# Prompt values of the sparse and memory attention as pairs of 64-column matmuls, two transposed buffers at a time

## Chip, core and metric

The kernel runs on one core of one Trainium2 chip. The metric is the device time of one launch in microseconds (us), and lower is better. "PE" is TensorE's matrix engine, "PEld" its weight loads, "DVE" VectorE, "ACT" ScalarE, "POOL" GpSimd, and "SP" the queue that issues nearly all of the DMAs.

## What is computed

The reference is one layer with three groups of heads side by side, for a prompt of 2048 tokens and for a sample batch of 8 sequences of 16 new tokens with a cache of 4096 keys. The change touches the last step of groups B and C for the prompt: probabilities times values.

```python
def sparse_block(q, qi, wi, q_pos, k, v, ki, k_pos, n_sel):      # group B, 4 heads of 64
    ...                                                          # top-256 of an indexer's scores
    s = jnp.einsum('bqhd,bqkhd->bqhk', q, ks) * (B_HD ** -0.5)
    p = jax.nn.softmax(s, axis=-1)
    return jnp.einsum('bqhk,bqkhd->bqhd', p, vs)

# group C, 4 heads of 64, 256 memory tokens
s_m = jnp.einsum('bqhd,bmhd->bhqm', q_m, mem_k) * (M_HD ** -0.5)
o_m = jnp.einsum('bhqm,bmhd->bqhd', jax.nn.softmax(s_m, axis=-1), mem_v)
o_m = o_m.reshape(bsz, t_len, M_WIDTH) * jax.nn.silu(z_m)

mix = jnp.concatenate([o_a, o_b, o_m], axis=-1)
y = x + mix @ w_out
```

## The kernel before

The 2176 tokens are 17 tiles of 128: tile 0 holds the sample's tokens, tiles 1 to 16 the prompt's. A first stage (up to about 1540 us) does the projections, group A and the indexer's selection. The second stage, the function `attention` (line 1677), does the rest, and the change lies in it. Several generators describe the work of that stage, and `weave` (line 173) interleaves them: each call of an engine through `Paced` (line 147) adds that class's own estimate of its duration to a clock, and the generator whose clock stands lowest is asked next. A Tile scheduler then fixes the order on each engine, so that one order of instructions per engine and per queue goes to the chip, and an engine waits at the next instruction of its list until that one can start.

The generators that matter here:

- `scores()` (line 1763) makes, for prompt tile g, the scores of 4 heads against 128·g keys and their exponentials in tiles `Sm`, and the scores against the memory in `Smm`.
- `values()` (line 1816) takes them up. A block is 128 queries by 128 keys of one head. Four blocks (two heads h, two key blocks c) are transposed on PE (`pt<-cf,Sm`, one call of 128x128 each), copied by ACT or DVE in turn into a buffer `PT` (two such buffers), and then multiplied with the values `Vt` (`mvt` for the memory). The multiplication is one call a key block: 128 value columns, which are two heads of 64, against 256 columns of `PT`, which are the probabilities of both heads. The result is 128x256, and half of it (one head's values under the other head's probabilities) is never read. The products of a buffer are queued behind the next buffer's transposes (the variable `late`). `hp` counts pairs of heads, `part` is 0 for group B and 1 for the memory.
- `outputs()` (line 1910) multiplies with `w_out` (`py<-woh,mixh` and so on, 24 calls a tile) once `values()` has stored a tile's `mixT`. It runs over the prompt tiles 1 to 16 and last over tile 0, the sample's, which it can start when the sample is done.
- `sample()` (line 1462) streams the sample's cache in 72 steps: 4 pairs of sequences with 17 key pieces each, and then 4 steps for the memory. A step has scores (`py` or `pi<-skt,bd`), an exponential, two transposes (`<-cf,SP`), a copy into `sPT`, and values two steps later (`<-svt,sPT`). These matmuls are 32 columns wide and lie in four column groups of the array. After the 68th and after the 72nd step the rows are gathered back out of a scratch tensor: 32 small DMAs `sPT<-os_d` on SP (line 1656), then a product with the gate and a store to `mix_d` (line 1660). The gather overwrites the tile `sPT` that the next step's copy needs.

Of the kernel before, what the change touches and what calls it, by code (L numbers as in the profile page):

```python
# [5 lines left out]
F32 = mybir.dt.float32  # L6
# [3 lines left out]
AF = mybir.ActivationFunctionType  # L10
OP = mybir.AluOpType
# [195 lines left out]
def build(tc, nc, a):  # L207
# [3 lines left out]
    V, S, G, T = (Paced(e, n, log) for e, n in ((nc.vector, "V"), (nc.scalar, "S"), (nc.gpsimd, "G"), (nc.tensor, "T")))  # L211


    cpool = ctx.enter_context(tc.tile_pool(name="const", bufs=1))
# [6 lines left out]
    ident = C("ident")  # L221
# [31 lines left out]
                                            ("glog", "beta", "gc", "ngc", "egc", "esuf", "last"))  # L253
    lasts = cpool.tile([128, 32], F32, name="lasts")
    hist = cpool.tile([128, 12, 3], F32, name="hist")
    Sst = cpool.tile([128, 4, 128], F32, name="Sst")
    V.memset(Sst, 0.0)
    cw = cpool.tile([128, 48], F32, name="cw")
    nc.sync.dma_start(cw, a["conv_w"])
    V.tensor_scalar(cw, cw, 0.5, None, op0=OP.mult)  # L260
# [21 lines left out]
    wpool = b1.enter_context(tc.tile_pool(name="wpool", bufs=2, side="right"))  # L282
    spool = b1.enter_context(tc.tile_pool(name="small", bufs=2))
    gpool = b1.enter_context(tc.tile_pool(name="gains", bufs=1))
    gains = gpool.tile([128, 224], F32, name="gains")
    nc.sync.dma_start(gains, a["gains"].to_broadcast([128, 224]))
    for o in (0, 128):
# [5 lines left out]
    po = b1.enter_context(tc.tile_pool(name="po", bufs=1, space=PSUM))  # L293
# [89 lines left out]
    def together(ins):  # L383

        return ExitStack() if ins is None else tc.issue_after(ins.ins)
# [865 lines left out]
    hp = b1.enter_context(tc.tile_pool(name="hp", bufs=2))  # L1251
# [55 lines left out]
    for gi in range(len(GROUPS)):  # L1307
        t = [[t_step(4 * gi + h, 0), t_step(4 * gi + h, 1)] for h in range(4)]
        n = [n_step(gi, pi) for pi in (1, 0, 2, 3, 4, 5)]
        steps += [i_step(gi)] + t[0] + n[:1] + t[1] + n[1:3] + t[2] + n[3:4] + t[3] + n[4:]  # L1310
    loaded, ready = [], []
# [365 lines left out]
    def attention(first):  # L1677
        with ExitStack() as b3:
# [5 lines left out]
            op = pool(b3, "op", 1, side="right")  # L1684
            py = pool(b3, "py", 2, side="right", space=PSUM)
            kv = pool(b3, "kv", 1)
            ap = pool(b3, "ap", 1)
            pt_ = pool(b3, "pt", 2, space=PSUM)
            ps_ = pool(b3, "ps", 1, space=PSUM)
            po_ = pool(b3, "po", 1, space=PSUM)  # L1690
# [5 lines left out]
            ready = []  # L1696
            M = sample_tiles(sp)
            sms = Slots(*((ap, "Sm%d" % i) for i in range(NS)))
            HALF = 1024

            class sx:
                name = "sx"
# [113 lines left out]
            def values():  # L1816


                for g in range(1, NT):
                    rows = slice(128 * g, 128 * g + 128)  # L1820
                    gate = ap.tile([128, 512], F32, name="gate")
                    nc.sync.dma_start(gate, gate_d[rows, :])
                    mixT = ap.tile([128, 4, 128], F32, name="mixT")
                    for part in range(2):
                        po = po_.tile([128, 512], F32, name="po").rearrange("p (a q) -> p a q", q=256)
                        nb = (g, 2)[part]
                        for hp in range(2):
                            j = 5 * (g - 1) + (4 if part else 2 * hp + 1)
                            yield from until(lambda: len(ready) > j)
                            yield -ready[j]["at"]  # L1830
                            if part:
                                blocks = [(h, c, ready[j]["x"][0][0][0][:, (2 * hp + h) * 256 + 128 * c:][:, :128], mvt[:, c])
                                          for c in range(2) for h in range(2)]
                            else:
                                blocks = [(h, c, ready[j - 1 + h]["x"][0][128 * c // HALF][0][:, 128 * c % HALF:][:, :128], Vt[:, c])
                                          for c in range(g) for h in range(2)]
                            late = None
                            for i in range(0, len(blocks) + 4, 4):
                                b = blocks[i:i + 4]
                                if b:  # L1840
                                    pt = pt_.tile([128, 4, 128], F32, name="pt")
                                    for x, (_, _, P, _) in enumerate(b):
                                        T.transpose(pt[:, x, :], P, ident)
                                    c = b[-1][1]
                                    if not part and ((c + 1) * 128 % HALF == 0 or c == g - 1):
                                        sms.free += [ready[j - 1 + h]["x"][0][128 * c // HALF][1] for h in range(2)]
                                    PT = ap.tile([128, 4, 128], F32, name="PT", bufs=2)
                                    if i // 4 % 2:
                                        V.tensor_copy(PT[:, :len(b)], pt[:, :len(b)])
                                    else:  # L1850
                                        S.activation(PT[:, :len(b)], pt[:, :len(b)], AF.Copy)
                                    yield 1
                                if late:
                                    yield 1
                                    for x, (_, c, _, Vb) in enumerate(late[0][::2]):
                                        T.matmul(po[:, hp], Vb[:, 128 * hp:128 * hp + 128], late[1][:, 2 * x:2 * x + 2, :].rearrange("p h q -> p (h q)"),
                                                 start=c == 0, stop=c == nb - 1, skip_group_check=True)
                                    yield 1
                                late = (b, PT)
                            count["v"] += hp if part else 2  # L1860
                        j = 5 * (g - 1) + (4 if part else 3)
                        den = ready[j]["x"][1]
                        V.reciprocal(den, den)
                        V.tensor_scalar(den, den, 0.5, None, op0=OP.mult)
                        gp = gate[:, 256 * part:256 * part + 256]
                        g3 = gp.rearrange("p (h d) -> p h d", d=64)
                        V.tensor_tensor(g3, g3, den[:, :, None].to_broadcast([128, 4, 64]), op=OP.mult)
                        yield 1
                        pt = pt_.tile([128, 4, 128], F32, name="pt")
                        for i in range(2):  # L1870
                            T.transpose(pt[:, i, :], gp[:, 128 * i:128 * i + 128], ident)
                        yield 1
                        mp = mixT[:, 2 * part:2 * part + 2]
                        S.activation(mp, pt[:, :2], AF.Copy)
                        yield 1
                        for h in range(2):
                            r = slice(64 * h, 64 * h + 64)
                            V.tensor_tensor(mp[r], po[r, :, 128 * h:128 * h + 128], mp[r], op=OP.mult)
                    nc.sync.dma_start(mixT_d[512:, rows].rearrange("(k p) t -> p k t", p=128), mixT)
                    count["o"] = g  # L1880

# [106 lines left out]
```

## Time and profile before

| What | Value |
|---|---|
| Median of 3 runs | 2322.36 us (2319.55 to 2326.96) |
| The profiled execution | 2319.37 us, of which 2317.5 us is the span from the first to the last instruction |
| PE busy over the span | 2041.4 us (88%), 13451 matmul instructions |
| PEld / DVE / ACT / POOL busy | 73% / 72% / 56% / 18% |
| Mean granted TensorE clock | 0.944 of full speed |
| DMA | 453.17 MB, 196 GB/s in the mean |
| The second stage's values, `po<-PT,Vt` | 544 instructions, 146.4 us busy |

An fp32 call stands as two MATMUL instructions in the profile, so the 544 instructions are 272 calls. A matmul's end is modelled: consecutive ones overlap in the rows, so the time that one costs is read from the start of one to the start of the next. The profile gives no chain of work that ended last for this kernel, so the path has to be read from starts and waits.

### The profile page before, as it was taken

What the parts mean: (1) busy time and instruction counts of PE and PEld (TensorE: products, weight loads), DVE (VectorE), ACT (ScalarE), POOL (GpSimd) and SP (SyncE); (2) the same over time, 40 slices, a digit from 0 to 9 for tenths busy, and PEclk for the clock granted to TensorE, in tenths of its full rate; (3) what the DMA queues carried; (4) which work ended last, traced back from release to release, by engine and by line L of the source; (5) the groups of instructions that cost most, each with busy time, mean ns of one, the idle gap of its engine ahead of it and who ended that gap; (6) DMA issues with size and microseconds to landing.
All of it is one profiled execution on the core that took longest, in us unless ns stands there. A gap on an engine that the chain in (4) does not pass through costs nothing.

```text
span 2317.5 us, 42207 instructions
## 1 busy us (share of the span) xinstructions
PE 2041.4 (88%) x13451; PEld 1682.0 (73%) x13451; DVE 1672.7 (72%) x6603; ACT 1293.4 (56%) x3193; POOL 420.7 (18%) x494
## 2 busy tenths in 40 slices
PE   4877878788899998999899999989999989999897
PEld 3655646677688987888788888856677666777675
DVE  4766655576888788889898897777677786646552
ACT  3455555455545565666666664457557666545441
POOL 3232413111111111111121012133111221110000
PEclk9987979798999998999899999999999999999898
DMA  7687667775544546556555656367777766766321
GB/s 233 181 250 212 215 149 236 193 249 188 196 161 164 177 154 233 182 192 226 184 206 178 227 195 218 119 201 245 237 222 236 237 215 222 244 217 193 109 65 61
DMA packets 323528, 453.17 MB, mean 196 GB/s; under 512 B 81760, under 2 KB 230880, under 8 KB 303840
## 3 DMA queue, kind: packets, MB, share of 16 engines
q1 hardware_dynamic: 322976, 449.32, 61.1%
q8 instruction: 109, 1.79, 0.3%
q0 software_dynamic: 320, 1.06, 0.3%
q14 instruction: 123, 1.01, 0.1%
HBM read 344.53 MB, written 105.75 MB: 194 GB/s over the span
## 4 chain that ended last, share of the span: by engine, by line


## 5 line engine op out<-in xcount | busy, mean ns | idle before, releaser
L169 PE MATMUL pp<-wh,xh 128*128 128x256 f32 (+1 forms) x952 | 287.3, 302 | 8.6 <-ACT xh L169 3.6
L169 PE MATMUL pp<-wl,xh 128*128 128x256 f32 (+1 forms) x952 | 278.7, 293 | 2.2 <-POOL wl L169 2.2
L169 PE MATMUL pp<-wh,xl 128*128 128x256 f32 (+1 forms) x952 | 277.9, 293 | 1.7 <-DVE xl L169 1.7
L169 PE MATMUL pp<-xh,wh 128*128 128x384 f32 (+1 forms) x640 | 249.2, 389 | 7.7 <-ACT q L169 3.0
L169 ACT ACTIVATE relu<-pi 128x512 f32<-128x512 f32 (+3 forms) x340 | 183.5, 545 | 117.5 <-PE pi L169 70.6
L169 PE MATMUL pp<-xh,wl 128*128 128x384 f32 (+1 forms) x640 | 242.7, 380 | 2.7 <-DMA wl<-wd2l 1.7
L169 DVE SCALAR_TENSOR_TENSOR score<-relu,w,score 128x512 f32<-128x512 f32 (+3 forms) x304 | 220.8, 728 | 31.6 <-ACT relu L169 18.0
L169 PE MATMUL pp<-xl,wh 128*128 128x384 f32 (+1 forms) x640 | 242.4, 379 | 0.0
L169 PEld LDWEIGHTS pp<-wh,xh 128*128 128x128 f32 x952 | 184.2, 194 | 12.8 <-ACT xh L169 5.1
L169 PEld LDWEIGHTS pp<-wl,xh 128*128 128x128 f32 x952 | 184.4, 194 | 5.7 <-POOL wl L169 2.6
L169 PEld LDWEIGHTS pp<-wh,xl 128*128 128x128 f32 x952 | 183.5, 193 | 4.8 <-DVE xl L169 2.6
L169 ACT ACTIVATE junk<-score,tf 128x1024 bf16<-128x1024 f32 (+11 forms) x126 | 142.6, 1132 | 72.0 <-DVE tf L169 47.1
L169 PE MATMUL po<-PT,Vt 128*128 128x256 f32 x544 | 146.4, 386 | 0.5 <-ACT PT L169 0.3
L169 POOL TENSOR_TENSOR Lm<-Lp,cf 128x256 f32<-128x256 f32 (+1 forms) x120 | 85.4, 712 | 312.1 <-PE pb L169 289.0
L169 PE MATMUL pi<-kstack,qst 128*128 128x512 f32 (+3 forms) x304 | 128.5, 431 | 14.6 <-ACT relu L169 12.1
L169 PEld LDWEIGHTS pp<-xh,wh 128*128 128x128 f32 x640 | 125.6, 196 | 17.5 <-ACT q L169 3.7
L169 PEld LDWEIGHTS pp<-xh,wl 128*128 128x128 f32 x640 | 125.3, 196 | 15.0 <-POOL wl L169 2.2
L169 PE MATMUL py<-woh,mixh 128*128 128x512 f32 x272 | 123.9, 456 | 12.2 <-ACT mixh L169 12.0
L169 PEld LDWEIGHTS pp<-xl,wh 128*128 128x128 f32 x640 | 125.8, 197 | 8.2
L169 POOL TENSOR_TENSOR wl<-wr,wh 128x512 fp32r<-128x512 f32 (+1 forms) x61 | 80.4, 1328 | 214.3 <-ACT wh L169 198.4
L169 PE MATMUL py<-woh,mixl 128*128 128x512 f32 x272 | 111.0, 409 | 3.5 <-POOL mixl L169 3.3
L169 PEld LDWEIGHTS po<-PT,Vt 128*128 128x128 f32 x544 | 95.3, 190 | 21.2 <-issue 6.7
(421 smaller groups left out, 5490.7 us busy)
## 6 DMA issues: line engine op xcount, KB each, us to landing
skt<-in_kT SPq DMA_DIRECT2D x128, 256.0 KB
svt<-in_v SPq DMA_DIRECT2D x128, 256.0 KB
nraw<-in_x SPq DMA_DIRECT2D x34, 256.0 KB
xres<-in_x SPq DMA_DIRECT2D x34, 256.0 KB
part_d<-xres SPq DMA_DIRECT2D x34, 256.0 KB
xres<-part_d SPq DMA_DIRECT2D x34, 256.0 KB
out_y<-xres SPq DMA_DIRECT2D x34, 256.0 KB
mixr<-mixT_d SPq DMA_DIRECT2D x33, 256.0 KB
```

What stands on the lines that cost most here:

```text
L169: return f(*args, **kw)
```

## The change

`visit` queues the products of up to two buffers in one run, and `tc.issue_after` (through `together`) ties the second buffer's run behind the first's. A product is now one head: 64 value columns against the 128 columns of that head's probabilities, written to partitions 0 to 63 (h = 0) or 64 to 127 (h = 1) of `po`. So each 128x256 call becomes two 64x128 calls that lie in different halves of the array's columns. There are three `PT` buffers instead of two, products are queued when three buffers wait, and what is left over at the end of a part is queued then; the list `late` now runs over both pairs of heads. The product with the gate is one instruction of 128x256 instead of two of 64x256. `Sst` moves to a pool that is closed before the second stage.

```diff
-    Sst = cpool.tile([128, 4, 128], F32, name="Sst")
-    V.memset(Sst, 0.0)
...
+    Sst = gpool.tile([128, 4, 128], F32, name="Sst")
+    V.memset(Sst, 0.0)
...
+                def visit(po, nb, late, n):
+                    lead = None
+                    for hp, b, PT in late[:n]:
+                        with together(lead):
+                            for x, (h, c, _, Vb) in enumerate(b):
+                                d = 64 * (2 * hp + h)
+                                ins = T.matmul(po[64 * h:64 * h + 64, hp, :], Vb[:, d:d + 64], PT[:, x, :],
+                                               start=c == 0, stop=c == nb - 1, skip_group_check=True)
+                        lead = ins
+                    del late[:n]
...
-                        po = po_.tile([128, 512], F32, name="po").rearrange("p (a q) -> p a q", q=256)
+                        po = po_.tile([128, 512], F32, name="po")[:, :256].rearrange("p (a q) -> p a q", q=128)
                         nb = (g, 2)[part]
+                        late = []
...
-                            late = None
-                            for i in range(0, len(blocks) + 4, 4):
+                            for i in range(0, len(blocks), 4):
...
-                                    PT = ap.tile([128, 4, 128], F32, name="PT", bufs=2)
+                                PT = ap.tile([128, 4, 128], F32, name="PT", bufs=3)
...
-                                if late:
-                                    yield 1
-                                    for x, (_, c, _, Vb) in enumerate(late[0][::2]):
-                                        T.matmul(po[:, hp], Vb[:, 128 * hp:128 * hp + 128], late[1][:, 2 * x:2 * x + 2, :].rearrange("p h q -> p (h q)"),
-                                                 start=c == 0, stop=c == nb - 1, skip_group_check=True)
-                                    yield 1
-                                late = (b, PT)
+                                late.append((hp, b, PT))
+                                yield 1
+                                if len(late) > 2:
+                                    visit(po, nb, late, 2)
+                                    yield 1
                             count["v"] += hp if part else 2
+                        yield 1
+                        visit(po, nb, late, len(late))
+                        yield 1
...
-                        for h in range(2):
-                            r = slice(64 * h, 64 * h + 64)
-                            V.tensor_tensor(mp[r], po[r, :, 128 * h:128 * h + 128], mp[r], op=OP.mult)
+                        V.tensor_tensor(mp, po, mp, op=OP.mult)
```

The order of the whole second stage moves, on every engine. Three places of it follow; `po` are the products in question, `pt<-cf,Sm` the transposes ahead of them, `svt`, `skt` and `SP` the sample's values, scores and transposes, `py<-wo` the output's products.

On PE, in the values of the last prompt tile (g = 16), before:

```order
L169 MATMUL po<-PT,Vt 128x256
L169 MATMUL ps<-mkst,qm 128x256 x4
L169 MATMUL po<-PT,Vt 128x256
L169 MATMUL pt<-cf,Sm 128x128 x4
L169 MATMUL po<-PT,Vt 128x256 x2
```

and in the changed kernel:

```order
L169 MATMUL po<-PT,Vt 64x128 x8
L169 MATMUL pt<-cf,Sm 128x128
L169 MATMUL pi<-skt,bd 32x256 x2
L169 MATMUL pt<-cf,Sm 128x128 x7
L169 MATMUL po<-PT,Vt 64x128 x8
L169 MATMUL pt<-cf,Sm 128x128 x4
```

Four transposes were followed by two products before; now up to eight narrow products stand together, and steps of the sample stand between them. Counted over the second stage, the 336 calls stood in 183 runs before, and the 672 narrow ones stand in 139 runs, of which 39 are whole runs of 8.

On PE, the end of the program from the last prompt tile's memory values on, before:

```order
L169 MATMUL pt<-cf,Smm 128x128 x8
L169 MATMUL pt<-cf,gate 128x128 x2
L169 MATMUL po<-PT,mvt 128x256 x4
L169 MATMUL py<-woh,mixh 128x512
L169 MATMUL py<-wol,mixh 128x512
```

and in the changed kernel:

```order
L169 MATMUL po<-PT,mvt 64x128 x8
L169 MATMUL pt<-cf,gate 128x128 x2
L169 MATMUL pi<-svt,sPT 32x128 x8
L169 MATMUL pi<-skt,bd 32x256 x4
L169 MATMUL pi<-cf,SP 128x128 x2
L169 MATMUL py<-woh,mixh 128x512
```

Before, the sample's last step stood two prompt tiles ahead of this place; now its last four steps stand behind it, the first of them ahead of the last prompt tile's output products.

On SP, around the second gather of the sample's rows, before:

```order
L1656 DMA sPT<-os_d 16x64 x28
L1657 DMA sPT<-gate_d 128x256
L1900 DMA xres<-part_d 128x512
L1822 DMA gate<-gate_d 128x512
L1660 DMA mix_d<-sPT 128x256
```

and in the changed kernel, from the first gather on:

```order
L1656 DMA sPT<-os_d 16x64 x31
L1657 DMA sPT<-gate_d 128x256
L1887 DMA mixT_d<-mixT 128x4x128
L1660 DMA mix_d<-sPT 128x256
L1929 DMA mixr<-mixT_d 128x4x128
```

Before, three prompt tiles' stores (`mixT_d`) still followed the second gather; now the last prompt tile's store stands behind the first gather, and nothing but the last stores and loads of the output follow the second one.

## Rows read from the trace of the kernel before

**Rows 1.** Windows: length; busy us of PE, PEld, DVE, ACT, POOL; granted clock; DMA share; GB/s.
```profile
1573.00:2140.00 567.00, 537.95 (x4094) 400.18 (x4094) 393.49 (x1313) 338.23 (x848) 92.17 (x82) 0.99 0.72 227
2140.00:2180.00 40.00, 31.06 (x218) 22.65 (x216) 18.65 (x61) 15.69 (x42) 3.26 (x3) 0.84 0.40 120
2180.00:2287.00 107.00, 103.27 (x593) 83.79 (x591) 55.36 (x152) 48.31 (x97) 6.38 (x5) 1.00 0.21 65
2287.00:2318.00 31.00, 15.17 (x54) 11.28 (x54) 4.32 (x8) 1.23 (x2) 1.27 (x1) 0.77 0.23 80
```

**Rows 2.** Waits of PE from 1573 to 2290 us: total, times, longest.
```profile
PE py L169 <- DMA svt<-in_v: 7.9, 8, 3.0
PE po L169 <- ACT PT L169: 1.3, 2, 1.0
```

**Rows 3.** The tiles `po` and `PT`: count, shortest, median and longest ns.
```profile
L169 PE MATMUL po<-PT,Vt x544: 377/379/535, 1573.6 to 2282.9; 128*128 128x256 f32 x182
L169 PE MATMUL po<-PT,mvt x128: 377/379/484, 1583.0 to 2286.5; 128*128 128x256 f32 x128
...
L169 ACT ACTIVATE PT<-pt x112: 361/597/628, 1573.1 to 2284.7; 128x512 f32<-128x512 f32 x104, 128x256 f32<-128x256 f32 x8
L169 DVE COPY PT<-pt x64: 411/685/693, 1607.0 to 2281.4; 128x512 f32<-128x512 f32 x56, 128x256 f32<-128x256 f32 x8
```

**Rows 4.** Timeline of PE: start us, length, instruction, count.
```profile
1902.39 1.02 PE L169 MATMUL po<-PT,Vt 128*128 128x256 f32 x4
1903.26 0.38 PE L169 MATMUL py<-cf,SP 128*128 128x128 f32 x2
1903.47 0.60 PE L169 MATMUL pt<-cf,qs 128*128 128x128 f32 x4
...
1907.28 0.64 PE L169 MATMUL py<-svt,sPT 128*32 128x128 f32 x16
1907.74 0.29 PE L169 MATMUL py<-smask,selb 128*32 128x256 bf16 x4
1907.85 0.61 PE L169 MATMUL py<-skt,bd 128*32 128x256 f32 x8
1908.40 1.13 PE L169 MATMUL po<-PT,Vt 128*128 128x256 f32 x4
```

**Rows 5.** Timeline of PE, the sample's values of steps 68, 69 and 72.
```profile
2150.06 0.43 PE L169 MATMUL pi<-svt,sPT 128*32 128x128 f32 x8 [1.32 <-ACT sPT L169]
...
2171.69 1.77 PE L169 MATMUL pi<-svt,sPT 128*32 128x128 f32 x14 [5.11 <-ACT sPT L169]
...
2188.94 0.64 PE L169 MATMUL pi<-svt,sPT 128*32 128x128 f32 x16
```

**Rows 6.** Timeline of SP's queue over the two gathers.
```profile
2153.79 0.38 SPq L1649 DMA_DIRECT2D os_d<-sO  x1
...
2171.25 0.32 SPq L1660 DMA_DIRECT2D mix_d<-sPT  x1
...
2192.22 14.07 SPq L1656 DMA_DIRECT2D sPT<-os_d  x28
...
2209.16 0.32 SPq L1660 DMA_DIRECT2D mix_d<-sPT  x1
```

**Rows 7.** Timeline of PE from the last values to the end.
```profile
2284.97 1.90 PE L169 MATMUL po<-PT,mvt 128*128 128x256 f32 x8
2294.00 0.80 PE L169 MATMUL py<-woh,mixh 128*128 128x512 f32 x1 [7.13 <-ACT mixh L169]
...
2302.85 0.60 PE L169 MATMUL pt<-cf,mixr 128*128 128x128 f32 x4
2304.19 0.50 PE L169 MATMUL py<-woh,mixh 128*128 128x512 f32 x1 [0.75 <-ACT mixh L169]
...
2309.86 0.19 PE L169 MATMUL pf<-cf,fail 128*1 128x1 f32 x2
```

**Rows 8.** Timeline of SP's queue, the last prompt tile's store.
```profile
2287.90 0.37 SPq L1879 DMA_DIRECT2D mixT_d<-mixT  x1
```

More of the change, by code (lines that the diff above doesn't have):

```diff
@@ L1836, in values @@
                                           for c in range(g) for h in range(2)]
-                            late = None
-                            for i in range(0, len(blocks) + 4, 4):
+                            for i in range(0, len(blocks), 4):
                                 b = blocks[i:i + 4]
[L1840 to L1846, printed above, removed]
-                                    PT = ap.tile([128, 4, 128], F32, name="PT", bufs=2)
[L1848 to L1851, printed above, removed]
-                                    yield 1
-                                if late:
-                                    yield 1
-                                    for x, (_, c, _, Vb) in enumerate(late[0][::2]):
-                                        T.matmul(po[:, hp], Vb[:, 128 * hp:128 * hp + 128], late[1][:, 2 * x:2 * x + 2, :].rearrange("p h q -> p (h q)"),
-                                                 start=c == 0, stop=c == nb - 1, skip_group_check=True)
-                                    yield 1
-                                late = (b, PT)
@@ new lines, in values @@
+                                pt = pt_.tile([128, 4, 128], F32, name="pt")
+                                for x, (_, _, P, _) in enumerate(b):
+                                    T.transpose(pt[:, x, :], P, ident)
+                                c = b[-1][1]
+                                if not part and ((c + 1) * 128 % HALF == 0 or c == g - 1):
+                                    sms.free += [ready[j - 1 + h]["x"][0][128 * c // HALF][1] for h in range(2)]
+                                PT = ap.tile([128, 4, 128], F32, name="PT", bufs=3)
@@ new lines, in values @@
+                                if i // 4 % 2:
+                                    V.tensor_copy(PT[:, :len(b)], pt[:, :len(b)])
+                                else:
+                                    S.activation(PT[:, :len(b)], pt[:, :len(b)], AF.Copy)
+                                late.append((hp, b, PT))
+                                yield 1
+                                if len(late) > 2:
+                                    visit(po, nb, late, 2)
+                                    yield 1
```

## Prediction

> **What bounds the kernel now.** The change lies in the second stage, so the first view is the table of windows. From 1573 us, when the prompt's values begin, to 2140 us PE is busy for 537.95 of 567 us (95%), and from 2180 to 2287 for 103.27 of 107 us (97%), at a granted clock of 0.99 and 1.00; DVE stands at 69% and ACT at 60% in the first of these, the DMA engines at 0.72 [rows 1]. So the stage moves at PE's pace. The second view, PE's waits, agrees: a few us on the sample's loads (7.9 us on `svt`), 1.3 us on the copies of transposed probabilities [rows 2]. Two short stretches are otherwise. Between 2140 and 2180 PE is busy for only 31.06 of 40 us and the clock is 0.84 [rows 1]: this is the end of the sample, where a copy into `sPT` waits for the gather and PE waits 5.11 us for the copy [rows 5, 6]. And the last 31 us after the last values are a chain of DMA, copy and products [rows 1, 7, 8], with PE half idle.
>
> **What a product costs, before and after.** The tile view counts 544 + 128 instructions, which are 336 calls at two each [rows 3]. Four of them in a row take from 1902.39 to 1903.26, 0.87 us, so a call of 256 columns takes 0.435 us, and all 336 take 146.2 us of PE [rows 4]. A narrow call streams 128 columns: 0.218 us if it stands alone. There are 672 of them, so all is lost unless two run at once. No row shows 64-column matmuls in two halves, but the sample's 32-column ones show four groups at once. Its 16 `svt` instructions are 8 calls of 128 columns; in file they would take 8 x 0.218 = 1.74 us, and they take 0.46 us, from 1907.28 to 1907.74, which is two rounds of 0.23 us [rows 4]. Its 8 `skt` instructions are 4 calls of 256 columns and take 0.55 us instead of 1.74 us, one round and 0.115 us [rows 4]. I therefore take 0.23 us for a round of two narrow calls, and the bounds are 0.218 us (nothing on top) and 0.435 us (one after the other). I choose the near end because these rows are of the same engine, type and column count.
>
> The 672 calls stand in 139 runs, and a run with an odd number wastes half a round: 367 rounds by count over the order shown above. They cost 367 x 0.23 = 84.4 us. Besides, the array changes between 128-wide and narrower use at each end of a run. Counted the same way, the changes of width rise from 224 to 455. The `skt` run carries 0.115 us beyond its one round, and 0.012 us of that is in the `svt` rounds too, so I take 0.10 us a change, with 0 and 0.2 us as bounds, since a change to 64 columns is in no row: 231 x 0.10 = 23.1 us. **PE gets 146.2 - 84.4 - 23.1 = 38.7 us back.**
>
> **The smaller parts.** One product with the gate in place of two of 64 partitions takes some 0.42 us off DVE 32 times; DVE is not what PE waits for, so I count it as nothing, and were that cover gone it would be worth 13 us at most. The copies into `PT` stay the same 112 on ACT and 64 on DVE at about 0.60 and 0.69 us [rows 3]. Their waits (1.3 us [rows 2]) stay or shrink: with three buffers a product begins further behind the transpose that it needs. A third buffer and the move of `Sst` cost no instruction in the stage. The front of the program up to 1573 us is the same.
>
> **What moves to the end.** This is the part that decides how much of the 38.7 us is seen. Before, the sample's last step ran at 2188.94, some 96 us before the last values ended at 2284.97 + 8 x 0.2175 = 2286.7 [rows 5, 7]. Now the prompt runs ahead of the sample in the order, and the sample's last four steps, its two gathers and its output stand behind the last values, where nothing covers them. Two gains come with that. Four steps of 1907.28 to 1908.40, 1.1 us each [rows 4], leave the front: 4.5 us. And the hole of 2140 to 2180 leaves it: PE was idle for 8.9 us there, where 5% would be 2, and the clock was low for a part [rows 1]; I take 11 us, between 7 and 13. So the last values end 38.7 + 4.5 + 11 = **54.2 us earlier**, at 2232.5.
>
> The end itself I add up from the rows. From the values of step 68 to those of step 69 it took 2150.06 to 2171.69, 21.6 us, for the first gather [rows 5]. From step 69 to step 72 it took 17.3 us, to 2188.94, with other products in between [rows 5]; here about half of the 24 output products stand there, at 0.23 us, so I take 13 us, between 9 and 17. From step 72 to the store of the gathered rows: 2188.94 to 2209.16, 20.2 us, of which 14.07 us are 28 DMA issues [rows 5, 6]. From such a store to the product that reads it: 2287.90 to 2294.00, 6.1 us [rows 7, 8]; the sample's has transposes in front, from 2302.85 to 2304.19, 1.3 us with a copy of some 0.7 us that the 6.1 hold already [rows 7], so 6.7 us. The 24 products after such a pause took 2294.00 to 2302.85, 8.9 us [rows 7]. From their end at 2309.86 to the end of the span: 7.6 us [rows 7]. Together 78.0 us from step 68. Step 68 stands ahead of the last values by 16 rounds, 26 transposes at 0.105 us [rows 4], a `skt` round of two halves and a dozen changes of width, about 9 us. So from the last values to the end it will be 69.0 us, where it was 2317.5 - 2286.7 = 30.8 us: **the end gets 38.2 us longer.**
>
> **The sum.** -54.2 + 38.2 = -16 us. Against the profiled execution, 2319.4 us, this is 2303.4 us, rounded 2303; the median of the runs shown lies 3 us higher than that execution.
>
> **Rivals.**
> *Pairs that overlap less (slower).* The place is each round of two 64-column calls. The point from which it decides: the front must save 38.2 us to pay for the longer end, so the rounds may cost 146.2 - 23.1 + 15.5 - 38.2 = 100.4 us, 0.274 us each. A pair that takes longer makes the kernel slower; at 0.33 us (half overlapped) it is 121 us and the kernel 2324 us; with no overlap at all the rounds cost 146.2 us and it ends near 2365 us. For it: two halves are in no row. Against it: four quarters overlap fully. TensorE: Matmul & The Clock Gate (the Trainium skill, Measured speedup vs the span model) gives 2.38 times for three column tiles, 0.79 of full; by that ratio a round would take an estimated 0.275 us and the kernel would stay where it is, and the `svt` row above speaks against it. Chance 0.13.
>
> *The room is not taken (no change).* PE's 38.7 us come back as idle time, because the sample's loads, DVE and the copies cannot run faster: 16 us of new waits, out of more than 650 us, are enough to end at 2319 us. For it: 7.9 us of waits on `svt` already, the DMA share of 0.72, DVE 69% [rows 1, 2]. Against it: PE is the one engine near full, and the sample's steps are now spread over a longer part of the stage. PSUM Bottleneck in TensorEngine Tiling (the Trainium skill) warns that evacuation becomes the limit once matmuls speed up; here the copies are 112 x 0.6 + 64 x 0.69 = 111 us on two engines over 714 us [rows 3]. Chance 0.17.
>
> *A shorter end (faster by more).* The waits on `svt` go (7.9 us), steps 69 to 72 take 9 us, and changes of width cost half: 8 + 4 + 12 us more, 2279 us. Chance 0.08.
>
> That the sample would not be last in spite of the order is excluded, since each engine follows its list.
>
> **How the numbers follow.** My forecast (PE saves about 39 us, the bare end takes back about two thirds of what the front gains) has a chance of 0.62; with 0.08 for the shorter end the kernel is faster with 0.70. A measurement of this kernel can tell 0.3% (7 us) from no change: unchanged 0.17, slower 0.13. The range begins a little below the shorter end, at 2276 us, and goes up to 2326 us, which takes in the unchanged case and the half overlapped pair; changes of width at 0.2 us would add 23 us to the forecast and reach the same end. No overlap lies outside.
>
> **What would show it.** Right: `po` instructions in pairs a few ns apart, runs of 8 calls in about 0.95 us; the last `po<-PT,mvt` near 2232 us; then a PE that waits some 12 us on `sPT` for the first gather, and again about 25 us between the sample's last values and its output's transposes, at a low granted clock; and some 69 us from the last values to the end. Wrong: pairs 0.2 us apart; more idle time of PE between 1600 and 2200 us than the 5% of before; or a sample whose last steps stand well ahead of the last values.

## The result and the profile after

| What | Value |
|---|---|
| Median of the changed kernel | 2284.4 us (2283.38 to 2285.57, 4 runs) |
| Median of the kernel before beside it | 2320.95 us (4 runs) |
| Ratio | 0.9838, 95% interval 0.9816 to 0.986, which is 33 to 43 us less |
| Profiled execution of the changed kernel | 2285.57 us, span 2283.8 us |

The kernel is faster by 36.5 us where 16 was forecast. The direction was right, and so were the overlap of the pairs and the longer end. What the new order does to the stage ahead of the last values was put far too low.

The windows of the changed kernel come first; the columns are as in [rows 1]. The second stage begins at 1575 us here, 2 us later than before, and the last values end at 2220.

```profile
1575.00:2140.00 565.00, 547.46 (x4747) 399.98 (x4750) 397.07 (x1333) 360.71 (x882) 97.24 (x83) 0.99 0.70 220
2140.00:2180.00 40.00, 38.86 (x367) 27.09 (x359) 23.39 (x70) 21.23 (x53) 2.56 (x2) 1.00 0.54 170
...
1575.00:2220.00 645.00, 623.68 (x5469) 454.11 (x5469) 439.50 (x1464) 397.00 (x975) 101.61 (x87) 0.99 0.68 214
2220.00:2283.00 63.00, 23.34 (x142) 14.82 (x142) 9.78 (x32) 4.24 (x11) 1.28 (x1) 0.70 0.24 74
```

PE is busy for 547.46 of 565 us, 97% where it was 95% [rows 1], and the hole of 2140 to 2180 is gone. From the first values to the last it is idle for 645 - 623.68 = 21.3 us. Before, the same stretch showed:

```profile
1573.00:2287.00 714.00, 672.28 (x4901) 506.63 (x4900) 467.50 (x1525) 402.24 (x986) 101.81 (x90) 0.98 0.62 196
```

That is 714 - 672.28 = 41.7 us of idle time. I call the first stretch the *front* and the rest up to the span's end the *end*. The front went from 712.9 to 644.2 us (first `po<-PT` to last, the latter from 2286.5 to 2219.7), and the end from 31.0 to 64.1 us.

The products in the tile view, which answers to [rows 3] (1088 + 256 instructions, 672 calls), and in the timeline of PE, which answers to [rows 4]:

```profile
L169 PE MATMUL po<-PT,Vt x1088: 272/273/476, 1575.5 to 2217.2; 128*64 128x128 f32 x182
L169 PE MATMUL po<-PT,mvt x256: 272/273/323, 1585.1 to 2219.7; 128*64 128x128 f32 x128
```

```profile
1993.89 0.40 PE L169 MATMUL py<-woh,mixh 128*128 128x512 f32 x1
1994.12 0.39 PE L169 MATMUL py<-wol,mixh 128*128 128x512 f32 x1
1994.35 0.40 PE L169 MATMUL py<-woh,mixl 128*128 128x512 f32 x1
1994.67 1.09 PE L169 MATMUL po<-PT,Vt 128*64 128x128 f32 x16
1995.70 0.54 PE L169 MATMUL pi<-svt,sPT 128*32 128x128 f32 x12
...
2208.97 0.43 PE L169 MATMUL po<-PT,Vt 128*64 128x128 f32 x2
2209.33 0.66 PE L169 MATMUL pt<-cf,Sm 128*128 128x128 f32 x4
...
2214.05 1.09 PE L169 MATMUL po<-PT,Vt 128*64 128x128 f32 x16
2215.07 0.66 PE L169 MATMUL pt<-cf,Sm 128*128 128x128 f32 x4
2215.66 0.66 PE L169 MATMUL po<-PT,Vt 128*64 128x128 f32 x8
2216.25 0.44 PE L169 MATMUL pi<-cf,SP 128*128 128x128 f32 x2
```

Eight calls take 1.02 us and four take 0.59 us (2214.05 to 2215.07, 2215.66 to 2216.25). The difference, 0.43 us, is two rounds, so a round of two calls costs 0.215 to 0.218 us and the pairs overlap in full; in the trace the instructions of a pair start 6 to 7 ns apart. What is left of a run is 1.02 - 4 x 0.218 = 0.15 us, and the product in front of a run takes 0.32 us instead of 0.23 (1994.35 to 1994.67). So a run carries 0.24 us, 0.12 us for each of its two changes of width.

The end in the timeline of PE, which answers to [rows 5, 7], and then in SP's queue [rows 6, 8]:

```profile
2210.52 0.43 PE L169 MATMUL pi<-svt,sPT 128*32 128x128 f32 x8
...
2218.83 1.14 PE L169 MATMUL po<-PT,mvt 128*64 128x128 f32 x16 [0.31 <-ACT PT L169]
2219.91 0.44 PE L169 MATMUL pt<-cf,gate 128*128 128x128 f32 x2
2232.73 1.77 PE L169 MATMUL pi<-svt,sPT 128*32 128x128 f32 x14 [12.39 <-ACT sPT L169]
...
2243.17 0.65 PE L169 MATMUL pi<-svt,sPT 128*32 128x128 f32 x16
...
2266.10 1.11 PE L169 MATMUL pt<-cf,mixr 128*128 128x128 f32 x4 [19.10 <-DMA mixr<-mix_d]
2267.96 0.79 PE L169 MATMUL py<-woh,mixh 128*128 128x512 f32 x1 [0.75 <-ACT mixh L169]
...
2275.59 0.19 PE L169 MATMUL pf<-cf,fail 128*1 128x1 f32 x2
```

```profile
2214.10 15.32 SPq L1656 DMA_DIRECT2D sPT<-os_d  x31
...
2246.25 11.94 SPq L1656 DMA_DIRECT2D sPT<-os_d  x26
...
2261.21 0.33 SPq L1660 DMA_DIRECT2D mix_d<-sPT  x1
```

The end runs as forecast: after the last values PE waits 12.39 us for the copy behind the first gather, whose 31 issues occupy the queue for 15.32 us, and later 19.10 us for the sample's rows, with the second gather's issues in it.

### The profile page after: what moved, and what is told of

Same layout as the page of the kernel before. It is cut to its first block, busy times and chain, and to the rows that moved or that the text cites. A ratio compares the mean times of both kernels' runs of the same rounds, so it can differ in the third digit from the quotient of the medians.

```text
span 2283.8 us, 43471 instructions
## 1 busy us (share of the span) xinstructions
PE 2006.2 (88%) x14123; PEld 1637.8 (72%) x14123; DVE 1651.3 (72%) x6571; ACT 1290.8 (57%) x3193; POOL 421.6 (18%) x494
## 4 chain that ended last, share of the span: by engine, by line
## 5 line engine op out<-in xcount | busy, mean ns | idle before, releaser
L169 PE MATMUL py<-wol,mixh 128*128 128x512 f32 x272 | 110.3, 405 | 0.0
L169 POOL TENSOR_TENSOR mixl<-mixr,mixh 128x512 fp32r<-128x512 f32 x33 | 42.3, 1281 | 328.1 <-ACT mixh L169 252.3
```

Source lines behind the costliest of these rows:

```text
L169: return f(*args, **kw)
```

## The experiments

On the chips of the experiments the unchanged first stage took 1579 to 1591 us and the kernel before 2332 to 2337 us. So totals are compared by their ratio to the kernel before on the same chip, and the traces by the lengths of front and end.

| Kernel | Ratio (95%) | Front | idle in it | End |
|---|---|---|---|---|
| before | 1 | 712.9 | 41.7 | 31.0 |
| changed | 0.9838 (0.9816 to 0.986) | 644.2 | 21.3 | 64.1 |
| wide_two | 0.9924 (0.9895 to 0.9953) | 684.1 | 26.1 | 42.5 |
| wide_order | 0.9956 (0.9925 to 0.9986) | 674.2 | 25.9 | 62.9 |
| narrow_one | 0.9956 (0.9931 to 0.9981) | 702.0 | 45.8 | 30.9 |
| in_file2 | 0.9963 (0.9941 to 0.9985) | 663.6 | 14.0 | 63.6 |
| fewer_stops | 1.0106 (1.0069 to 1.0142) | 646.9 | 18.5 | 129.5 |
| more_stops | 0.987 (0.9826 to 0.9915) | 686.0 | 42.3 | 31.7 |
| one_gather | 0.9771 (0.9736 to 0.9806) | 640.7 | 22.0 | 45.0 |
| mem_gather | 0.9721 (0.9689 to 0.9753) | 641.9 | 22.9 | 31.9 |
| before_gather | 0.9928 (0.9903 to 0.9953) | 707.4 | 36.9 | 30.8 |
| after_again (the changed kernel) | 0.9859 (0.9825 to 0.9894) | 645.7 | 24.4 | 64.1 |
| mg_y1 | 0.9775 (0.974 to 0.981) | 653.8 | 27.9 | 32.7 |
| three_all | 0.9735 (0.9699 to 0.977) | 648.4 | 28.0 | 31.7 |

Times in us. Where a text below turns a ratio into a time, it is the ratio times 2321 us. Front, idle time and end come from one traced execution of each kernel, up to 10 us away from that kernel's median (mg_y1: 2272 against 2282 us; wide_order: 2327 against 2322), and the rows of before and of the changed kernel were taken apart from the others, where before ran 0.5 to 0.7% slower. So differences of a few us between fronts are not told from noise.

### Is it the pairs or the queueing?

**wide_two** keeps the queueing and the third buffer and goes back to wide calls (with the `po` tile and the product with the gate as before):

```diff
-                            for x, (h, c, _, Vb) in enumerate(b):
-                                d = 64 * (2 * hp + h)
-                                ins = T.matmul(po[64 * h:64 * h + 64, hp, :], Vb[:, d:d + 64], PT[:, x, :],
+                            for x, (_, c, _, Vb) in enumerate(b[::2]):
+                                ins = T.matmul(po[:, hp], Vb[:, 128 * hp:128 * hp + 128], PT[:, 2 * x:2 * x + 2, :].rearrange("p h q -> p (h q)"),
...
```

> The changed kernel with its queueing (two buffers in a run, three buffers), but each product again one call of 128 x 256. Theory A (the gain is TensorE time of the narrow pairs, plus idle time that falls because the sample's steps are spread otherwise): the products cost 146 us again instead of about 106 with their changes of width, so some 38 us more than the changed kernel; the sample's last step has 6 wide products and 48 output products behind it, where the changed kernel has 0 and 37, so the end is a few us shorter: about 2318 us (2308 to 2328), as before. Theory B (the idle time falls because of the narrow pairs, in any order): 2340 to 2350 us. Theory C (the queueing and the third buffer bring the gain, the narrow pairs nothing): 2280 to 2292 us.

Measured: 0.9924, 17.6 us faster than before, between what theories A and C expected. So A was wrong in one point: the queueing brings something by itself. The front is 28.8 us shorter, 15.6 of it idle time, and the end 11.5 us longer.

**wide_order** writes the same wide calls but enters the narrow calls' estimate into `weave`, so that the order is nearly the changed kernel's (of the 4262 other matmul instructions of the stage 3778 stand in the same sequence on PE):

```diff
-                                ins = T.matmul(po[:, hp], ...
+                                ins = nc.tensor.matmul(po[:, hp], ...
...
+                                log.extend([("T", 214.0 * 0.62 + 3)] * 2)
...
```

> The changed kernel in its very order, but two narrow calls at a time are one call of 128 x 256 at the same place. Theory A: idle time stays at the changed kernel's 21 us up to the last values, the products cost 38 to 40 us more: about 2322 us (2316 to 2330). Theory B: the idle time goes back to before's 49 us: about 2349 us. Theory C: about 2284 us, as the changed kernel.

Measured: 0.9956, 2311 us, below what theory A expected (2316 to 2330) and far from B and C. The windows:

```profile
1588.00:2262.00 674.00, 648.15 (x4794) 499.94 (x4793) 460.86 (x1494) 399.11 (x975) 100.38 (x87) 0.99 0.65 204
2262.00:2324.00 62.00, 25.18 (x143) 15.59 (x142) 10.20 (x33) 3.74 (x10) 1.28 (x1) 0.71 0.25 75
```

Idle time in the front is 674 - 648.15 = 25.9 us without a single narrow product: it fell with the order, as A said and B denied. Against this kernel, the changed one's front is 28 to 30 us shorter (644.2 and 645.7 against 674.2) at an end that is 1 us longer; by the ratios the difference is 23 to 27 us (0.9859 and 0.9838 against 0.9956). That is what the pairs bring in an order that is nearly held fixed.

**narrow_one** puts the narrow pairs into the kernel before, one buffer at a time:

```diff
-                                    for x, (_, c, _, Vb) in enumerate(late[0][::2]):
-                                        T.matmul(po[:, hp], Vb[:, 128 * hp:128 * hp + 128], late[1][:, 2 * x:2 * x + 2, :].rearrange("p h q -> p (h q)"),
+                                    for x, (h, c, _, Vb) in enumerate(late[0]):
+                                        d = 64 * (2 * hp + h)
+                                        T.matmul(po[64 * h:64 * h + 64, hp, :], Vb[:, d:d + 64], late[1][:, x, :],
...
```

> The kernel before with narrow pairs, its queueing of one buffer at a time and two buffers kept. Some 60 more runs of products than in the changed kernel, so about 119 more changes of width at 0.093 us, 11 us more of TensorE; but the sample's last step has 124 narrow products and 91 output products behind it, so the end would be the 31 us of before and not 64. Theory A (idle time stays as before, 49 us): 2284 + 11 - 33 + 27 = 2289 us (2280 to 2298). Theory B (idle time falls as in the changed kernel): about 2262 us (2255 to 2270). Theory C (narrow pairs bring nothing): 2320 us or more.

Measured: 0.9956, which is 2311 us, 10 us faster than before and not 30: a miss for A (2280 to 2298) and B (about 2262). C's 2320 is nearest, but lies outside the interval (2305 to 2317). Idle time stays high at 45.8 us, as A said, and the end at 30.9. What A had wrong is the front: 702.0. This kernel has 575 changes of width where before had 224; at 0.12 us, 351 more cost 42 us, and 370 rounds cost 80.7 us, so of the 146.2 us of before only 23 are saved, and 11 of them show in the front, where idle time is also 4 us higher. My expectation counted from the changed kernel, whose front also holds the order's gain, and took only the idle time out of it. So pairs pay little when every buffer is a run of its own.

**in_file2** sorts the calls of a run by half:

```diff
-                    for hp, b, PT in late[:n]:
...
+                    flat = sorted(((hp, x, *v, PT) for hp, b, PT in late[:n] for x, v in enumerate(b)), key=lambda v: v[2])
```

> The changed kernel with the calls of a run sorted by the half of the array that they use, all of the lower half, then all of the upper: neighbours share a half and only one pair in a run can overlap, about 214 rounds of 0.22 us more. Theories A and B: 45 to 48 us more than the changed kernel, about 2331 us (2320 to 2340); a run of 8 calls takes some 1.65 us instead of 1.02. Theory C: no difference, 2284 us.

Measured: 0.9963, 24 to 29 us more than the changed kernel (0.9859 and 0.9838) where 45 were expected. A run of eight calls in this kernel's timeline:

```profile
2002.00 1.58 PE L169 MATMUL po<-PT,Vt 128*64 128x128 f32 x16
2003.51 0.65 PE L169 MATMUL pt<-cf,Sm 128*128 128x128 f32 x4
```

It takes 1.51 us, against 1.02 us with the halves in turn and 1.65 us expected: neighbours in one half go one after the other, but the upper half's calls begin while some of the lower half's are left (in the trace of this run single starts some 0.11 us apart up to 2002.49, then starts of both halves up to 2002.87, then single ones again). Theory C, that the pairs bring nothing, falls here and with wide_order.

### Is it the order?

After these four I held theory D: the pairs save some 30 us of PE, and the queueing's own effect is the order. `values()` stops less often, so `weave` lets the prompt run ahead of the sample; the sample's steps are spread over more of the front, and what PE no longer waits for there comes back as the bare end.

**fewer_stops** is the kernel before with two stops per buffer taken out and nothing else:

```diff
                                 if late:
-                                    yield 1
                                     for x, (_, c, _, Vb) in enumerate(late[0][::2]):
...
-                                    yield 1
                                 late = (b, PT)
```

> The kernel before (wide products, one buffer at a time, two buffers) with two of the three stops taken out of each buffer of the prompt's values, so that in the planner the prompt runs ahead of the sample; nothing else changes. The last dozen steps of the sample then stand behind the last values. Theory D (the gain of the queueing alone is the order: the sample is spread over more of the stage, so PE waits less in the front, and the bare end takes it back): idle time up to the last values falls from 42 us to 26 or less, the front falls by 30 to 50 us, the end grows by 60 to 80 us: slower than before, about 2345 us (2330 to 2365). Theory E (the longer runs and the third buffer make the gain, the order does not): idle time stays near 42 us and the front falls only by the steps that left it, some 12 x 1.5 = 18 us; 2365 us or more.

Measured: 1.0106, which is 2346 us. The windows:

```profile
1579.00:2226.00 647.00, 628.55 (x4478) 492.04 (x4478) 448.20 (x1428) 388.75 (x934) 102.00 (x89) 0.99 0.62 193
2226.00:2355.00 129.00, 57.54 (x487) 30.72 (x485) 25.57 (x102) 16.31 (x55) 1.80 (x2) 0.64 0.45 138
```

Idle time in the front falls to 18.5 us with wide calls, single buffers and no third one. So theory D holds for the idle time, and E falls. The front is as short as the changed kernel's, but 44 of the 66 us by which it shrinks are busy time (672.28 to 628.55), nearly all of which stands in the end now (57.54 us where it was 15.17). The end takes 129.5 us at a granted clock of 0.64. Both moves are larger than D had them (66 for 30 to 50, 98 for 60 to 80), and that the total came out as expected is partly luck.

**more_stops** is the opposite, the changed kernel with two stops more per buffer:

```diff
                                 yield 1
+                                yield 1
+                                yield 1
                                 if len(late) > 2:
```

> The changed kernel (narrow pairs, two buffers in a run, three buffers) with two stops more per buffer, so that the planner lets the sample run ahead as before: 140 narrow products and 90 output products stand behind its last step. Products by the measured prices: 369 rounds of 0.2185 us and 254 changes of width more than before at 0.119 us, 34 us less than before. Theory D: idle time in the front goes back to about 42 to 46 us, the end is again 31 us: front about 680, about 2289 us, near the changed kernel. Theory E: idle time stays at about 21 us, as in the changed kernel, and the short end comes on top: about 2265 us.

Measured: 0.987, which is 2291 us, as D said (2289) and not E (2265). The windows and the longest of PE's waits in the front:

```profile
1586.00:2272.00 686.00, 643.70 (x5571) 462.40 (x5567) 449.82 (x1489) 400.33 (x984) 102.66 (x89) 0.98 0.65 205
2272.00:2303.00 31.00, 15.52 (x58) 11.42 (x56) 3.92 (x7) 1.61 (x3) 1.27 (x1) 0.78 0.24 79
```

```profile
PE py L169 <- DMA svt<-in_v: 9.3, 8, 2.8
PE pi L169 <- DMA skt<-in_kT: 4.0, 3, 1.5
PE pt L169 <- ACT qs L169: 3.9, 4, 2.4
```

With the same narrow calls as the changed kernel, idle time is back at 686 - 643.7 = 42.3 us, first of all on the sample's loads, which take 9.3 us here and 3.6 us in the changed kernel. Against the changed kernel on such a chip (after_again) the front is 686.0 - 645.7 = 40.3 us longer (about 4 us of it are 33 more changes of width at 0.12 us), and the end 64.1 - 31.7 = 32.4 us shorter. So the order by itself is nearly a wash: 8 us by the stages, and the intervals of the two ratios overlap.

**before_gather** stores a step's rows in the order in which they are read back, so that a gather is one DMA and not 32, in the kernel before:

```diff
-    os_d = dpool.tile([2, 4, 128, 64], F32, name="os_d")
+    os_d = dpool.tile([2, 128, 256], F32, name="os_d")
...
-                    nc.sync.dma_start(os_d[kind2, p2], O[:, :64])
+                    for b2 in range(2):
+                        nc.sync.dma_start(os_d[kind2, 32 * p2 + 16 * b2:32 * p2 + 16 * b2 + 16].rearrange("q (h d) -> h q d", d=64), O[64 * b2:64 * b2 + 64, :64])
...
-                                nc.sync.dma_start(ot[16 * pb:16 * pb + 16, 64 * h:64 * h + 64], sv[pb])
+                        nc.sync.dma_start(ot, os_d[kind2])
```

> The kernel before with the single gather DMA alone (two stores per step in the order of the read). It measures the term of the prediction that the hole of 2140 to 2180 us is worth: there the first gather's 28 issues kept PE waiting, at a clock of 0.84, and I took 11 us (7 to 13) for it. If that is right: 11 us less than before, ratio 0.9953, and PE busy for over 37 of the 40 us after step 68. The end after the last values stays 31 us, since the second gather is covered. If the hole is refilled from elsewhere (PE waits for the same loads a little later): no difference. If the hole was dearer than I took it, as a part of the missing gain: 20 us or more, ratio 0.991.

Measured: 0.9928, which is 17 us (11 to 23) against the 11 that I had put down for the hole. Its window over the two gathers:

```profile
2148.00:2200.00 52.00, 50.11 (x408) 37.22 (x403) 34.57 (x115) 26.80 (x67) 5.12 (x5) 1.00 0.55 173
```

PE is busy for 96% at a full clock where it was busy for 78% at 0.84 [rows 1]. The lengths of the stage show only 6 us of it (738.2 against 743.9), but those are single executions on two chips, and the one of before_gather took 7.5 us more than its median (2328.76 against 2321.23). So the hole was worth 11 us or somewhat more, which is not what the forecast missed most.

### The bare end

**one_gather** is the same edit in the changed kernel.

> The changed kernel, but each step's output is stored to DRAM in the order in which it is read back, by two stores, so that a gather is one DMA instead of 32. In the changed kernel the 28 issues of a gather take 14 us of the queue, PE waits 12.4 us for the first one and the second lies between step 72 and the last store. If the bare end is made of these issues as I took it: 68 to 69 shrinks from 22.2 to about 10 us, step 72 to the store from 18.0 to about 6 us: 24 us less than the changed kernel, about 2260 us (2253 to 2268). If the wait for the first gather is only replaced by another (the loads of step 69, the planner's own 5 us): about 2272 us. If the landing and not the issues costs the time: 2284 us.

Measured: 0.9771, which is 2268 us, at the upper edge of what was expected. The end shrinks from 64.1 to 45.0 us. PE's timeline:

```profile
2215.51 0.43 PE L169 MATMUL pi<-svt,sPT 128*32 128x128 f32 x8
...
2226.20 0.65 PE L169 MATMUL pi<-svt,sPT 128*32 128x128 f32 x16 [0.75 <-ACT sPT L169]
...
2234.14 1.08 PE L169 MATMUL pi<-svt,sPT 128*32 128x128 f32 x16 [0.53 <-ACT sPT L169]
...
2251.20 1.12 PE L169 MATMUL pt<-cf,mixr 128*128 128x128 f32 x4 [7.73 <-DMA mixr<-mix_d]
```

From step 68 to step 69 it takes 10.7 us instead of 22.2, as expected, and the 12.39 us of waiting are gone. From step 72 to the store it takes 11.1 us (2234.14 to 2245.28 in SP's queue) where 6 were expected: the gather is issued only at 2242.28, 4 us after the last of the stores that it reads:

```profile
2237.28 1.06 SPq L1650 DMA_DIRECT2D os_d<-sO  x2
...
2242.28 0.33 SPq L1654 DMA_DIRECT2D sPT<-os_d  x1
...
2245.28 0.32 SPq L1658 DMA_DIRECT2D mix_d<-sPT  x1
```

**mem_gather** also puts the four memory steps first (and so loads the memory's queries first):

```diff
-        steps = [(0, p, c) for p in range(4) for c in range(17)] + [(1, p, 0) for p in range(4)]
+        steps = [(1, p, 0) for p in range(4)] + [(0, p, c) for p in range(4) for c in range(17)]
...
-                    if kind and p == 0:
-                        bd = yield from queries(qm_d)
+                    if j == 4:
+                        bd = yield from queries(qn_d)
...
```

> As the one with a single gather DMA, and the sample's four memory steps are put first instead of last, so that their gather lies in the middle of the stage and only one gather stands in the bare end; the last steps of the sample follow each other without a break. 128 runs of products instead of 139, 417 changes of width instead of 455: some 4 us less of TensorE. The end after the last values is then about three steps of 5 us, 6 us to the store, 6.8 to the product, 7.6 and 8.3: about 42 us instead of 64: about 2255 us (2245 to 2264). If the break at the first gather was not what made the end long: as the single gather, 2260 us.

Measured: 0.9721 (0.9689 to 0.9753), which is 2256 us, 65 us less than before. It beats both kernels.

```profile
1591.00:2233.00 642.00, 619.10 (x5557) 453.83 (x5556) 435.90 (x1439) 396.34 (x978) 99.52 (x84) 0.99 0.69 218
2233.00:2264.00 31.00, 16.19 (x85) 11.63 (x81) 6.11 (x15) 2.16 (x6) 1.50 (x1) 0.82 0.31 94
```

The front is the changed kernel's (642 us, 22.9 idle) and the end is before's (31 us): the 33 us that the longer end had taken back are all there again. I had expected 42 us of end; the sample's last steps stand beside the last values and not behind them, so only its last product chain is bare.

**after_again** is the changed kernel, run beside the two that follow and before_gather.

> The changed kernel once more, beside the others on one chip: ratio to before 0.9838 as first measured (0.981 to 0.987); the last values some 64 us ahead of the span's end, idle time in the front 21 us (17 to 26).

Measured: 0.9859, with front 645.7, idle 24.4 and end 64.1 us: the first result repeats.

**mg_y1** takes mem_gather and lets the sample run a little further ahead:

```diff
-                        yield 1500.0
+                        yield 1
```

> The kernel with narrow pairs, the memory steps first and the single gather, with the sample's own stop of 1500 ns per step taken down to the planner's least, so that the sample runs ahead by about 8 narrow products more. 449 changes of width instead of 417, 133 runs instead of 128: 4 us more of TensorE. The end cannot shrink below 31 us, where it is already. If the sample's pace only trades idle time in the front against the bare end: within 5 us of the kernel without it, ratio 0.972 to 0.975. If there is still bare end to cover: 0.968.

Measured: 0.9775, a miss: 12 us slower than mem_gather by the ratios, with intervals that overlap a little. The end had nothing left to give (32.7 us), idle time in the front is 5 us higher, and of the rest of the front's 12 us about 4 us are the 32 more changes of width; the remainder is open, and the two traces come from two chips.

**three_all** puts all three buffers of mem_gather into one run, with one stop more ahead of it:

```diff
                                 if len(late) > 2:
-                                    visit(po, nb, late, 2)
+                                    yield 1
+                                    visit(po, nb, late, 3)
```

> As the best so far (memory steps first, single gather, narrow pairs), but all three buffers go in one run, so that no buffer is free for the next copy while a run goes on: 107 runs instead of 128, 354 rounds instead of 359, 419 changes of width as 417 there. If the third buffer is what keeps PE from waiting for the copies: PE's waits on the copies rise from about 2 us to 15 us or more (some 45 long runs of 0.3 us at least) and the kernel is 10 to 20 us slower, ratio 0.977 to 0.981. If the other streams cover the copies: equal, 0.970 to 0.974.

Measured: 0.9735, the same as mem_gather within the intervals. The waits on the copies stay small:

```profile
PE po L169 <- ACT PT L169: 1.7, 3, 0.8
PE po L169 <- DVE PT L169: 1.7, 2, 1.1
```

So a buffer that is free during a run is not what keeps PE supplied. That the other streams' work covers the copies is how I read it.

## Why the prediction was right in direction and wrong in size

**The pairs overlap (right).** Rounds were put at 0.23 us and cost 0.215 to 0.218. The rival that they overlap less is out. The 2.38 times that TensorE: Matmul & The Clock Gate gives (the Trainium skill, Measured speedup vs the span model) for three column tiles, 0.79 of full, would have made it an estimated 0.275 us; this trace, with 0.218 us for two halves in fp32, doesn't follow that ratio. The price of that rival was also summed wrongly: half overlapped rounds of 121 us are 36.7 us more than 84.4, which makes 2340 us and not 2324, so the range up to 2326 did not take them in.

**Changes of width (too low).** 0.10 us were taken and 0.12 us measured. With that, 146.2 - 367 x 0.218 - 231 x 0.12 = 38.5 us would still be as forecast (38.7), but in a nearly fixed order the front gives 28 to 30 us. The 9 us between come out when the trace is counted from each matmul's start to the next one's, waits left out. The wide products then take 140.2 us in the front before and 141.0 in wide_order, not 146.2, since one row of two calls had stood for all. And with wide calls the changed order has 186 changes of width in the front, where the changed kernel has 444, so the pairs add 258 and not 231. 141.0 - 367 x 0.218 - 258 x 0.12 = 30 us. The same count shows where it goes: the narrow products take 102.6 us, 38.4 less, but the calls around them 12.3 us more, and 139 runs at 0.09 us on the way in would be 12.5.

**What the order does to the front (wrong, and the main miss).** The four steps that leave the front (4.5 us) and the hole of 2140 to 2180 (11 us) made 15.5 us. With the products held wide, the queueing and its order take 712.9 - 674.2 = 38.7 us off the front, and with narrow ones the order alone takes 40.3 us (more_stops against after_again). The forecast looked at the one stretch where PE visibly waited and took the idle time elsewhere ("where 5% would be 2") for given. But of before's 41.7 us of idle time only 8.9 us lie in that stretch [rows 1]. The rest is spread over waits of up to three us, on the sample's loads [rows 2] and on other streams, of which these are examples, first before and then in the changed kernel:

```profile
PE py L169 <- ACT mixh L169: 4.2, 3, 2.3
...
PE py L169 <- DMA svt<-in_v: 3.6, 3, 1.7
PE py L169 <- ACT mixh L169: 1.7, 1, 1.7
PE po L169 <- ACT PT L169: 1.1, 3, 0.4
```

About half of the idle time goes with the order: 25.9 us with wide calls, 21.3 with narrow ones, 18.5 in fewer_stops, and 42.3 when the order is put back. That it goes because the sample's steps stand further apart fits the waits on `svt` (7.9 to 3.6 us) but is not shown by itself. Idle time so falls by 16 to 20 us where the forecast held 7 of it (8.9 less 2), which is 9 to 13 of the missing 23 us. The remainder is PE's busy time, which is 24 us lower in wide_order than before (672.28 to 648.15); four steps at 1.1 us and a full clock in place of 0.84 for 31 us make some 9 of these. Counted from start to start, 13.3 us lie in the sample's `skt`, `svt` and `SP` (98.2 us before, 84.9 in wide_order, the four steps included), 5.9 in the scores (121.2 and 115.3) and 4.1 in the other transposes (115.8 and 111.7), while the output's products (189.2 and 189.4) and the values stay as they were. Why those calls follow each other faster than the 9 us account for stays open.

**The longer end (right in kind, 5 us too long).** 69.0 us were forecast and 64.1 measured, twice. Piece by piece: 22.2 us from step 68 to step 69 (21.6 forecast), 10.4 from there to step 72 (13), 18.0 to the store (20.2), 6.75 to the product (6.7), 7.6 for the 24 products (8.9) and 8.2 to the end of the span (7.6).

**The sum.** Forecast -38.7 - 15.5 + 38.2 = -16. By the stages of the runs, with wide_order between the two kernels, it is -30 for the pairs, -38.7 for the order's front and +33.1 for the end, together -35.6, as the two spans' stages differ (743.9 and 708.3). Two errors of opposite sign, 9 us too much for the pairs and 23 too little for the order, and 5 us of the end make the difference of 20. That the forecast was not further off is luck: the pairs' error hid a part of the order's.

**Other rivals.** That the room is not taken: PE is busy for 97% of the front, and its waits on the copies stay at 1.1 us there, so the limit that PSUM Bottleneck in TensorEngine Tiling (the Trainium skill) warns of doesn't appear here. The shorter end (2279 us) was nearest in number, but only partly for its reasons: waits on `svt` fell from 7.9 to 3.6 us and the steps 69 to 72 took 10.4 us, while changes of width cost more than forecast and not half.

## What to carry to other kernels

Two half-width matmuls at once came near their full factor only in long runs here: each run paid 0.24 us for going in and out, and the same pairs saved 10 us with runs of mostly four calls and 23 to 30 us with runs of up to eight. Where a planner weaves streams, any change to one stream's stops moves the others, so count the idle time of the whole stretch and not its visible holes, and look at which stream ends last. A part that then stands bare at the end is worth mending by itself: reordering the sample's steps and making a gather one DMA gave 27 to 32 us by the ratios, nearly as much as the change.

## What the runs showed of the hardware that I had not expected

Two column halves in fp32 overlap without loss: eight calls in two halves take 1.02 us, of which four rounds of 0.218 us are exactly four single calls. Going to 64 columns and back costs 0.24 us a run, and as much whether one or eight calls stand in it (2208.97 to 2209.33, 0.36 us for one call, is 0.218 + 0.15; 0.59 us for four is 2 x 0.218 + 0.15, and 1.02 us is 4 x 0.218 + 0.15). And calls that are queued half by half still overlap in part: 1.51 us for eight, where all one after the other would be 8 x 0.218 + 0.15 = 1.89 us.
